# A hybrid attention and linear-attention layer: parts of the columns of w_in kept in DRAM by the first token group

## The chip, the cores and the metric

One Trainium2 chip, one of its cores. The metric is the device time of one execution in microseconds (us), median over runs; the profile is of one further execution.

## What is computed

One layer of a decoder trunk, for 1024 prompt tokens with 16 meta tokens in front of them and for 64 sample tokens (8 sequences of 8). All data are float32. Cut to what matters here:

```python
h = rms_norm(x, norm1)
z = einsum('btd,de->bte', h, w_in)      # w_in: 1024 x 2320
# columns of z: q 512, k 128, v 128, gq 256, gk 256, gv 512, g_low 16, og 512
a = window_attention(rms_norm(q), rms_norm(k), v)   # softmax over 128 keys, 8 heads
o, s = gla_chunked(gq, gk, gv, log_decay(g_low))    # gated linear attention, 4 heads
x = x + concat(a, rms_norm(o) * silu(og)) @ w_o
x = x + swiglu(rms_norm(x), w_gate, w_up, w_down)
```

## The kernel before, in words

**Parts.** TensorE multiplies float32 operands in one pass after each was split in two parts: `hi`, the value rounded to the format fp32r, and `lo`, the rest (`raw - hi`). A product is three matmuls (`mm3`, L102 to L107: hi by hi, hi by lo, lo by hi). Every weight chunk is therefore loaded as `raw`, rounded on ScalarE (`nc.scalar.copy`, L99) and subtracted on VectorE (L100). That is `load_split` (L92 to L101). A chunk of 128 x 1024 has 512 KB, and so has each of its two parts. The tiles `raw` have 3 buffers; `hi` and `lo` have 4 each (`rawpool`, `wpool`) in the stage of this change; a buffer of `hi` and `lo` is free again when the last matmul that reads it is done.

**Token groups.** The tokens are worked on in three groups of 3 tiles (`NG`, `tiles`): group 0 is the sample tokens with the meta tokens and two tiles of the prompt, groups 1 and 2 are three tiles of 128 tokens each. For each group `in_proj(g)` (L348 to L594) runs the input projection in column blocks: kv with g_low (272 columns), gq, gk (256 each), q, gv, og (512 each). q, gv and og are taken in 4 chunks of 256 rows by 512 columns (`token_major`, L366 to L386), gq and gk in 2 chunks of 512 rows by 256 columns each (L490 to L500). So each group loads and splits the same columns of w_in again: 16 chunks without kv. `PAIRS` (L30) takes two chunks at a time, and in turn: (chunk 0, tile 0), (1, 0), (0, 1), (1, 1), (0, 2), (1, 2), and then chunks 2 and 3. The two chunks of a pair thus come free almost together, at the pair's end.

**What sets the order.** `merge` (L978 to L1004) is a planner that runs while the program is built: it interleaves the steps of the input projection, of the output projection, of the attention (`attention_prompt`, L605, and `attention_sample`, L810) and of the linear attention (`gla_prompt`, L705, with `level_factors` at L678, and `gla_sample`, L869), from costs and waits that each step states. TensorE's order is the one that `merge` writes. On the other engines and on the DMA queues the scheduler of the kernel language sets the order when the program is built; each then runs its instructions in that fixed order, and an instruction that waits holds all behind it.

**Queues.** Loads of weights and inputs are issued on SP (`nc.sync.dma_start`, L83 for `raw`, L217 to L220 for the sample tokens' caches and states, L229 for x). GpSimd (POOL) issues a few stores (L442 to L446, L959, L1009 to L1012, L1086), makes the masks of `constants2` (L256) and computes the inverse roots of the norms (`rstd`, L162 to L166). A DRAM pool named `dram` is there already: `kvd` (L234) and `x1d` (L1015) are written and read back.

Of the kernel before, what the change touches and what calls it, by code (L numbers as in the profile page):

```python
# [8 lines left out]
F32 = mybir.dt.float32  # L9
# [8 lines left out]
P = 128  # L18
# [12 lines left out]
LAT = (1.34, 1.18, 1.23, 1.23, 1.2)  # L31
SPARSE, SHARE = 2.0, 1.0
POOL_HALVES = ((0, 1), (1,), (1,))
C_Q, C_K, C_V, C_GQ, C_GK, C_GV, C_GL, C_OG = 0, 512, 640, 768, 1024, 1280, 1792, 1808


@with_exitstack
def hymba_step(ctx: ExitStack, tc: tile.TileContext, x_prompt, x_sample, cache_k, cache_v, state_gla, meta,
               norm1, w_in, q_norm, k_norm, sinks, w_g2, b_g, gla_norm, w_o, norm2, w_gate, w_up, w_down,
               y_prompt, y_sample, nck_p, ncv_p, nst_p, nck_s, ncv_s, nst_s):  # L40
    nc = tc.nc
# [15 lines left out]
    dram = ctx.enter_context(tc.tile_pool(name="dram", bufs=1, space=bass.MemoryType.DRAM))  # L57

    def big(name):
        return psb.tile([P, 512], F32, tag="big", name=name)  # L60
# [4 lines left out]
    w_in_v = w_in.rearrange("(k p) e -> p k e", p=P)  # L65
# [10 lines left out]
    def load_raw(srcs, nk, n, name):  # L76

        raw = (rawpool[-1] if nraw[0] % 4 == 3 else rawpool[0]).tile([P, 1024], F32, tag="raw", name=f"raw_{name}")
        nraw[0] += len(rawpool) > 1
        c = 0  # L80
        for s in srcs:
            w = s.shape[-1]
            nc.sync.dma_start(raw[:, 0:nk * n].rearrange("p (k e) -> p k e", k=nk)[:, :, c:c + w], s)  # L83
            c += w
        return raw

    def parts(name):
        pool = wpool[nsplit[0] % 10 >= 4] if len(wpool) > 1 else wpool[0]
        nsplit[0] += len(wpool) > 1
        return (pool.tile([P, 1024], F32R, tag="hi", name=f"hi_{name}"),  # L90
                pool.tile([P, 1024], F32R, tag="lo", name=f"lo_{name}"))

    def load_split(srcs, nk, n, name, raw=None):

        if raw is None:
            raw = load_raw(srcs, nk, n, name)
        hi, lo = parts(name)
        raw_, hi_, lo_ = (a[:, 0:nk * n].rearrange("p (k e) -> p k e", k=nk) for a in (raw, hi, lo))
        nc.scalar.copy(hi_, raw_)  # L99
        last_lo[0] = nc.vector.tensor_tensor(lo_, raw_, hi_.bitcast(F32), op=ALU.subtract)  # L100
        return hi_, lo_  # L101

    def mm3(ps, lhs, rhs, first, last):
        (lh, ll), (rh, rl) = lhs, rhs
        nc.tensor.matmul(ps, lh, rh, start=first, stop=False)  # L105
        nc.tensor.matmul(ps, lh, rl, start=False, stop=False)  # L106
        nc.tensor.matmul(ps, ll, rh, start=False, stop=last)  # L107

    def mm2(ps, lhs, rhs, first, last):

        nc.tensor.matmul(ps, lhs, rhs[0], start=first, stop=False)
        nc.tensor.matmul(ps, lhs, rhs[1], start=False, stop=last)
# [38 lines left out]
    def tiles(g):  # L151
        return [3 * g - 1 + i for i in range(3)]
# [195 lines left out]
    def in_proj(g):  # L348

        hi8, hi, lo = hT[0][:, :, 0:P], hT[0][:, :, 64:], hT[1]  # L350
# [15 lines left out]
        def token_major(pieces, n, name, ps, order, after=None, sample_only=False):  # L366

            ps.extend(big(f"{name}{i}")[:, 0:n] for i in range(3))
            w = {}
            for step, (b, i) in enumerate(order):  # L370
                if b not in w:
                    w[b] = kv_w.pop(0) if kv_w else load_split([s[:, 2 * b:2 * b + 2, :] for s in pieces], 2, n, name)
                wh, wl = w[b]
                sl = slice(i * P, i * P + P)
                for k in range(2):
                    kk = 2 * b + k
                    rhs, ends = (wh[:, k, :], wl[:, k, :]), (kk == 0, kk == KC - 1)
                    if sample_only and g == 0 and i == 0:
                        mm2(ps[i], hi8[:, kk, :], rhs, *ends)
                    else:  # L380
                        mm3(ps[i], (hi[:, kk, sl], lo[:, kk, sl]), rhs, *ends)
                yield 6 * n / 2400.0
                if step % 3 == 2 and pend:
                    yield from pend.pop(0)
                if after:
                    yield from after(b, i)  # L386

        def into_hT(x, i, pool=()):
            sl = slice(i * P, i * P + P)
            for hf in range(2):  # L390
                transposed(x[i], P, n1T, hi[:, :, sl], lo[:, :, sl], (hf,), pool)
                if g == 0 and x is xt and i == 0:
                    ks = slice(hf * 4, hf * 4 + 4)
                    nc.gpsimd.tensor_copy(hi8[:, ks, 0:64], lo[:, ks, 0:64])
                yield 0.45

        kv_w = []
        if g == 0:
            for i, t in enumerate(tiles(g)):
                normed(xt[i], xt[i], P, f"1_{t}")  # L400
                if i == 0:
                    next(cols1)
                yield from into_hT(xt, i, POOL_HALVES[i])
                if i < 2:
                    kv_w.append(load_split(None, 2, 272, "kv", kv_raw[i]))
# [5 lines left out]

        ps = []
        yield from token_major(kv_src, 272, "kv", ps, PAIRS)
        GR[g]["lokv"] = last_lo[0]
        kns, gls, rks = [], [], []
# [74 lines left out]
        for nm, c0 in (("gq", C_GQ), ("gk", C_GK)):  # L490
            ps = [big(f"{nm}{pr}")[:, 0:384] for pr in range(2)]
            for k0 in range(0, KC, 4):
                wh, wl = load_split([w_in_v[:, k0:k0 + 4, c0:c0 + 256]], 4, 256, nm)
                for pr in range(2):
                    bs = slice(pr * P, pr * P + P)
                    for k in range(4):
                        mm3(ps[pr], (wh[:, k, bs], wl[:, k, bs]), (hi[:, k0 + k, :], lo[:, k0 + k, :]),
                            k0 + k == 0, k0 + k == KC - 1)
                    yield 12 * 0.163
                if pend:  # L500
                    yield from pend.pop(0)
            for i, t in enumerate(tiles(g)):
                yield need(lambda: done["G"] >= t + 2 - 4)
                a = R[t][nm] = work.tile([P, 2, P], F32, tag=nm, bufs=4, name=nm)
                for pr in range(2):
                    p1 = ps[pr][:, i * P:(i + 1) * P]
                    if nm == "gq":
                        nc.scalar.activation(a[:, pr, :], p1, AF.Copy, scale=0.125)
                    else:
                        nc.scalar.copy(a[:, pr, :], p1)  # L510
# [4 lines left out]

        ps = []
        yield from token_major([w_in_v[:, :, C_Q:C_Q + 512]], 512, "q", ps, PAIRS, sample_only=True)
        qns, rqs = [], []
        rows = [slice(0, 64 if t < 0 else P) for t in tiles(g)]
# [37 lines left out]

        ps = []
        yield from token_major([w_in_v[:, :, C_GV:C_GV + 512]], 512, "gv", ps, PAIRS)
        for i, t in enumerate(tiles(g)):  # L560
            yield need(lambda: done["G"] >= t + 2 - 3)
            gv = R[t]["gv"] = work.tile([P, 512], F32, tag="gv", bufs=3, name="gv")
# [8 lines left out]
        def after(b, i):  # L571
            if b == 3 and g < NG - 1:
                yield from into_hT(GR[g]["xnext"], i)
# [9 lines left out]
        for i, t in enumerate(tiles(g)):  # L583
            x, s = ps[i], sg[rows[i], i, :]
# [505 lines left out]
    def projections():  # L1090
        for g in range(NG):
            yield from in_proj(g)
            done["P"] += 3
# [430 lines left out]
    for c, pairs in enumerate(CHUNKS):  # L1524
        first, last = c == 0, c == len(CHUNKS) - 1
        W = W + blocks_W((1,)) if first else blocks_W(pairs)
        for tp in range(4):
# [6 lines left out]
            for j, m in enumerate(DOWN):  # L1534
# [6 lines left out]
                a = Y[tp][m]  # L1541
# [57 lines left out]
```

## Time and profile before

| | |
|---|---|
| median of 3 runs | 1252.57 us (1247.94 to 1252.75) |
| the profiled execution's own time | 1251.81 us |
| its span, first to last instruction | 1250.0 us |
| mean granted clock of TensorE | 0.985 of full |
| instructions | 23188 |
| DMA over the span | 183.17 MB |

The page gives for each engine its busy time and share of the span. Matmuls are pipelined: a matmul counts as busy from its start to its modelled end, so that several overlap, and an idle time of TensorE in the trace is a real stop. The three input projections stand at about 17 to 118 us (group 0), 124 to 251 us (group 1) and 254 to 373 us (group 2); attention and linear attention run in between.

### The profile page before, as it was taken

The numbers are of one execution on the slowest core, as the hardware profiler recorded it, in microseconds if no ns is written. First come the engines' busy times: TensorE is split into PE (matmuls) and PEld (weight loads), VectorE is DVE, ScalarE is ACT, GpSimd is POOL, SyncE is SP. The second block draws the span as 40 slices with busy tenths as digits, with TensorE's granted clock in tenths as the row PEclk, the third lists the DMA queues.
The fourth block names the chain that finished last, engine by engine and source line by source line (L and its number), as shares of the span: only waits on it lengthen the run. The fifth ranks groups of instructions, "written<-read, shape, count | busy, mean of one in ns | idle before, by whom it ended". The sixth has DMA issues, their size and how long they took to land.

```text
span 1250.0 us, 23188 instructions
## 1 busy us (share of the span) xinstructions
PE 1202.7 (96%) x9190; PEld 1066.3 (85%) x9190; DVE 873.2 (70%) x1742; ACT 514.7 (41%) x933; POOL 415.7 (33%) x360
## 2 busy tenths in 40 slices
PE   6999899999999999899999999999999979999997
PEld 6877788778777778789999999999999958888886
DVE  6746987698679876756667656666666666667786
ACT  5634665566566454433234323333332344112200
POOL 6212202131211101215434443544354433334653
PEclk9998999999999999989999999999999999999999
DMA  6723423242323544314435434442544486576545
GB/s 186 237 79 92 121 69 94 54 123 86 101 69 100 165 170 154 116 51 137 128 113 170 154 97 143 154 146 85 180 137 127 147 311 260 211 268 253 213 182 177
DMA packets 145178, 183.17 MB, mean 147 GB/s; under 512 B 15675, under 2 KB 113374, under 8 KB 145054
## 3 DMA queue, kind: packets, MB, share of 16 engines
q1 hardware_dynamic: 95438, 130.83, 32.0%
q10 hardware_dynamic: 47792, 43.98, 10.9%
q0 software_dynamic: 1840, 6.88, 1.6%
q8 instruction: 72, 1.18, 0.4%
q14 instruction: 36, 0.29, 0.1%
HBM read 131.86 MB, written 50.86 MB: 146 GB/s over the span
## 4 chain that ended last, share of the span: by engine, by line
PE 52%; issue 20%; POOL 13%; DVE 8%; ACT 4%; DMA 2%; SPq 0%; POOLq 0%; ACTq 0%; DVEq 0%
PE pd L106 6%; PE pd L107 5%; PE pd L105 5%; PE pw L105 2%; PE pw L106 2%; PE pw L107 2%; POOL raw_wu L1267 2%; PE pf L107 2%; PE pf L105 1%; PE pf L106 1%; POOL raw_wg L1265 1%; ACT hi_wg L1246 1%; PE gv L105 1%; DVE uo L1247 1%; POOL raw_wg L1264 1%
## 5 line engine op out<-in xcount | busy, mean ns | idle before, releaser
L105 PE MATMUL pd<-hi_wd,u 128*128 128x512 f32 x312 | 122.7, 393 | 5.0 <-ACT hi_wd L1246 5.0
L106 PE MATMUL pd<-lo_wd,u 128*128 128x512 f32 x312 | 123.4, 396 | 1.5 <-DVE lo_wd L1247 1.5
L107 PE MATMUL pd<-hi_wd,u 128*128 128x512 f32 x312 | 122.5, 393 | 0.0
L1246 ACT CAST hi_wg<-raw_wg 128x1024 fp32r<-128x1024 f32 (+1 forms) x44 | 41.4, 942 | 139.5 <-PE pf L106 65.9
L1247 DVE TENSOR_TENSOR uo<-u,uo 128x512 fp32r<-128x512 f32 x74 | 77.7, 1056 | 25.4 <-ACT uo L1246 24.0
L1543 DVE TENSOR_TENSOR y<-y,pd 128x512 f32<-128x512 f32 x112 | 73.5, 682 | 27.1 <-PE pd L107 27.1
L1247 DVE TENSOR_TENSOR lo_wu<-raw_wu,hi_wu 128x1024 fp32r<-128x1024 f32 (+1 forms) x44 | 49.2, 1119 | 55.8 <-ACT hi_wu L1246 55.8
L1246 ACT CAST hi_wd<-raw_wd 128x1024 fp32r<-128x1024 f32 x42 | 43.0, 1051 | 97.6 <-PE pd L107 38.4
L1246 ACT CAST uo<-u 128x512 fp32r<-128x512 f32 x74 | 44.7, 620 | 80.1 <-POOL u L1371 39.4
L105 PEld LDWEIGHTS pd<-hi_wd,u 128*128 128x128 f32 x312 | 58.9, 189 | 19.2 <-ACT hi_wd L1246 5.9
L106 PEld LDWEIGHTS pd<-lo_wd,u 128*128 128x128 f32 x312 | 59.0, 189 | 15.3 <-DVE lo_wd L1247 2.8
L1264 POOL TENSOR_TENSOR raw_wg<-raw_wg 128x512 f32<-128x512 f32 x11 | 18.4, 1669 | 160.6 <-DVE lo_wg L1247 135.4
L107 PEld LDWEIGHTS pd<-hi_wd,u 128*128 128x128 f32 x312 | 59.0, 189 | 12.6
L1247 DVE TENSOR_TENSOR lo_wg<-raw_wg,hi_wg 128x1024 fp32r<-128x1024 f32 (+1 forms) x44 | 48.9, 1112 | 27.8 <-ACT hi_wg L1246 27.8
L1247 DVE TENSOR_TENSOR lo_wd<-raw_wd,hi_wd 128x1024 fp32r<-128x1024 f32 x42 | 61.1, 1466 | 7.8 <-ACT hi_wd L1246 7.7
L1246 ACT CAST hi_wu<-raw_wu 128x1024 fp32r<-128x1024 f32 (+1 forms) x44 | 41.3, 938 | 52.9 <-POOL raw_wu L1265 28.4
L590 POOL TENSOR_SCALAR sg<-sg 128x512 f32<-128x512 f32 (+1 forms) x9 | 14.1, 1564 | 133.9 <-ACT sg L589 133.9
L106 PE MATMUL pw<-lo_wo,hThi 128*128 128x512 f32 x128 | 51.2, 400 | 2.7 <-DVE lo_wo L100 2.7
L105 PE MATMUL pw<-hi_wo,hThi 128*128 128x512 f32 x128 | 52.2, 408 | 0.0
L107 PE MATMUL pw<-hi_wo,hTlo 128*128 128x512 f32 x128 | 50.9, 398 | 0.0
L1264 POOL TENSOR_TENSOR raw_wu<-raw_wu 128x512 f32<-128x512 f32 x11 | 14.2, 1291 | 91.6 <-DVE lo_wu L1247 91.6
L1410 ACT ACTIVATE g<-g 128x544 f32<-128x544 f32 x44 | 28.9, 657 | 22.8 <-DVE g L1300 18.9
(714 smaller groups left out, 4248.4 us busy)
## 6 DMA issues: line engine op xcount, KB each, us to landing
ud<-uo ACTq DMA_DIRECT2D x74, 512.0 KB, 4.4
u<-ud SPq DMA_DIRECT2D x40, 896.0 KB, 6.2
raw_wo<-in_w_o_dram SPq DMA_DIRECT2D x24, 512.0 KB, 3.8
raw_wu<-in_w_up_dram SPq DMA_DIRECT2D x22, 512.0 KB, 3.8
raw_wg<-in_w_gate_dram SPq DMA_DIRECT2D x22, 512.0 KB, 4.5
raw_wd<-in_w_down_dram SPq DMA_DIRECT2D x22, 512.0 KB, 4.1
raw_q<-in_w_in_dram SPq DMA_DIRECT2D x12, 512.0 KB, 5.0
raw_gv<-in_w_in_dram SPq DMA_DIRECT2D x12, 512.0 KB, 3.6
```

The source lines that it names most:

```text
L105: nc.tensor.matmul(ps, lh, rh, start=first, stop=False)
L106: nc.tensor.matmul(ps, lh, rl, start=False, stop=False)
L107: nc.tensor.matmul(ps, ll, rh, start=False, stop=last)
L590: nc.gpsimd.tensor_scalar(s, s, 2.0 ** 60, None, op0=ALU.min)
L1246: nc.scalar.copy(hi, src)
L1247: nc.vector.tensor_tensor(lo, src, hi.bitcast(F32), op=ALU.subtract)
L1264: nc.gpsimd.tensor_tensor(a22, a21, a22, op=ALU.add)
L1265: nc.gpsimd.tensor_tensor(a21, a11, a21, op=ALU.subtract)
L1267: nc.gpsimd.tensor_tensor(a12, a12, a11, op=ALU.subtract)
L1410: nc.scalar.activation(a, a, AF.Silu)
L1543: tt(a, a, ps, op=ALU.add)
```

## The change

Group 0 loads and splits its chunks as before, and then also stores both parts of 16 of them (q, gv, og: 4 chunks each; gq, gk: 2 each) to tiles in DRAM, with DMAs that GpSimd issues. Groups 1 and 2 don't load `raw` for these chunks and don't split: they load the two parts straight into buffers of `hi` and `lo`, with DMAs on SP. The chunks of kv are treated as before, and so is w_o. The diff, whole:

```diff
+KEPT = ("q", "gv", "og")
...
-    def load_split(srcs, nk, n, name, raw=None):
-
+    kept = {}
+
+    def load_split(srcs, nk, n, name, raw=None, key=None):
+
+        if key in kept:
+            hl = parts(name)
+            for a, d in zip(hl, kept[key]):
+                nc.sync.dma_start(a[:, 0:nk * n].bitcast(F32), d)
+            return tuple(a[:, 0:nk * n].rearrange("p (k e) -> p k e", k=nk) for a in hl)
         if raw is None:
             raw = load_raw(srcs, nk, n, name)
         hi, lo = parts(name)
         raw_, hi_, lo_ = (a[:, 0:nk * n].rearrange("p (k e) -> p k e", k=nk) for a in (raw, hi, lo))
         nc.scalar.copy(hi_, raw_)
         last_lo[0] = nc.vector.tensor_tensor(lo_, raw_, hi_.bitcast(F32), op=ALU.subtract)
+        if key:
+            kept[key] = [dram.tile([P, nk * n], F32, name=f"{key}{i}") for i in range(2)]
+            for a, d in zip((hi, lo), kept[key]):
+                nc.gpsimd.dma_start(d, a[:, 0:nk * n].bitcast(F32))
         return hi_, lo_
...
-                    w[b] = kv_w.pop(0) if kv_w else load_split([s[:, 2 * b:2 * b + 2, :] for s in pieces], 2, n, name)
+                    w[b] = kv_w.pop(0) if kv_w else load_split([s[:, 2 * b:2 * b + 2, :] for s in pieces], 2, n, name,
+                                                                            key=f"{name}{b}" if name in KEPT else None)
...
-                wh, wl = load_split([w_in_v[:, k0:k0 + 4, c0:c0 + 256]], 4, 256, nm)
+                wh, wl = load_split([w_in_v[:, k0:k0 + 4, c0:c0 + 256]], 4, 256, nm, key=f"{nm}{k0}")
```

## Rows read from the trace of the kernel before

**Rows 1.** The page, section 1: TensorE's busy time, share of the span, instructions.
```profile
PE 1202.7 (96%) x9190; PEld 1066.3 (85%) x9190; DVE 873.2 (70%) x1742; ACT 514.7 (41%) x933; POOL 415.7 (33%) x360
```

**Rows 2.** Busy time by stretch: length; PE, PEld, DVE, ACT, POOL; PEclk; DMA share; GB/s.
```profile
20.00:50.00 30.00, 29.66 (x176) 27.36 (x176) 22.83 (x79) 21.33 (x49) 9.55 (x16) 1.00 0.97 299
50.00:85.00 35.00, 35.00 (x203) 28.26 (x202) 19.86 (x40) 17.28 (x29) 8.99 (x9) 1.00 0.37 105
85.00:112.00 27.00, 27.00 (x221) 21.33 (x219) 13.71 (x40) 6.93 (x17) 2.02 (x1) 0.81 0.23 60
112.00:160.00 48.00, 43.11 (x527) 36.39 (x527) 42.14 (x145) 31.58 (x79) 14.67 (x18) 0.96 0.39 115
160.00:240.00 80.00, 80.00 (x799) 63.76 (x801) 58.00 (x194) 44.04 (x100) 9.63 (x12) 1.00 0.26 75
240.00:290.00 50.00, 46.92 (x564) 39.30 (x553) 45.70 (x163) 37.78 (x100) 16.17 (x17) 1.00 0.34 102
290.00:375.00 85.00, 85.00 (x859) 68.07 (x858) 62.52 (x206) 47.97 (x105) 10.82 (x12) 1.00 0.29 88
```

**Rows 3.** Waits of TensorE, 112 to 380 us: us in total, times, longest.
```profile
PE pa L741 <- DVE Dt L692: 1.4, 1, 1.4
...
PE pk L458 <- DVE AD L702: 0.6, 1, 0.6
PE pst L770 <- DVE mx L623: 0.5, 1, 0.5
PE pk L458 <- ACT glT L455: 0.4, 1, 0.4
...
PE pgl L454 <- DVE mx L623: 0.4, 1, 0.4
PE pb L759 <- DVE Dt L692: 0.4, 1, 0.4
```

**Rows 4.** VectorE in order of time, 138 to 153 us: start, us, instruction.
```profile
138.22 1.21 DVE L100 TENSOR_TENSOR lo_gq<-raw_gq,hi_gq 128x1024 fp32r<-128x1024 f32 x1
139.35 0.27 DVE L690 TENSOR_TENSOR qd<-Dt,gq 128x128 f32<-128x128 f32 x1
...
146.91 1.22 DVE L100 TENSOR_TENSOR lo_gk<-raw_gk,hi_gk 128x1024 fp32r<-128x1024 f32 x1
...
151.28 1.22 DVE L100 TENSOR_TENSOR lo_gk<-raw_gk,hi_gk 128x1024 fp32r<-128x1024 f32 x1
```

**Rows 5.** Busy time by stretch, one stretch of group 1 (columns as in Rows 2).
```profile
154.00:157.40 3.40, 3.40 (x13) 2.96 (x13) 3.34 (x14) 0.67 (x3) 0.00 (x0) 0.50 0.42 137
```

**Rows 6.** ScalarE's instructions of line 99 from 112 to 375 us: min, median, max ns.
```profile
L99 ACT CAST hi_q<-raw_q x8: 1044/1046/1058, 148.2 to 302.6; 128x1024 fp32r<-128x1024 f32 x8
```

**Rows 7.** The tile hi_q of group 0: ns min, median, max; first and last start.
```profile
L111 PE MATMUL q<-hi_q,hThi x8: 389/389/397, 47.8 to 56.4; 128*128 128x512 f32 x8
...
L100 DVE TENSOR_TENSOR lo_q<-raw_q,hi_q x4: 1219/1225/1226, 40.4 to 49.9; 128x1024 fp32r<-128x1024 f32 x4
```

**Rows 8.** ScalarE in order of time, at 138 us.
```profile
137.94 0.84 ACT L687 ACTIVATE Dt<-Dt 128x768 f32<-128x768 f32 x1 [0.26 <-DVE Dt L686]
```

**Rows 9.** The page, section 3, GpSimd's DMA queue: packets, MB, share of 16 engines.
```profile
q0 software_dynamic: 1840, 6.88, 1.6%
```

**Rows 10.** The tile x1d: issues on GpSimd of 512 KB stores, ns min, median, max.
```profile
L1086 POOL DMA_DIRECT2D x1d<-xr x8: 531/608/640, 424.8 to 512.8; - x8
```

**Rows 11.** SP in order of time, one load of a raw chunk.
```profile
22.77 0.37 SPq L83 DMA_DIRECT2D raw_gq<-in_w_in_dram  x1
```

**Rows 12.** DMA issues from 0 to 400 us: count, KB each, median us to landing.
```profile
raw_q<-in_w_in_dram SPq DMA_DIRECT2D x12, 512.0 KB, 5.0
raw_gv<-in_w_in_dram SPq DMA_DIRECT2D x12, 512.0 KB, 3.6
```

**Rows 13.** The tile hi_gv of group 2: its last matmuls' row (columns as in Rows 7).
```profile
L107 PE MATMUL gv<-hi_gv,hTlo x24: 387/390/398, 323.6 to 343.7; 128*128 128x512 f32 x24
```

**Rows 14.** GpSimd in order of time, 59 to 62 us.
```profile
59.84 0.20 POOL L164 TENSOR_SCALAR rq<-msq 128x8 f32<-128x8 f32 x1 [7.03 <-DVE msq L533]
...
61.86 1.83 POOL L164 TENSOR_SCALAR rq<-msq 128x8 f32<-128x8 f32 x1
```

## The prediction

> **What bounds the kernel now.** I began with the page: TensorE is busy 96% of the span, every other engine 70% or less [rows 1]. So a change that only unloads VectorE and ScalarE can pay no more than the stops of TensorE that they cause, in the stretches where their work goes. Second, I read busy time by stretch [rows 2]. From 50 to 112 us (most of group 0), from 160 to 240 and from 290 to 375 us TensorE never stops, whatever VectorE does. It stops in two stretches, the starts of groups 1 and 2: 48.00 - 43.11 = 4.9 us from 112 to 160, and 50.00 - 46.92 = 3.1 us from 240 to 290. There VectorE is nearly full (42.14 of 48 and 45.70 of 50). These 8.0 us, with the clock that they may cost, are the most that the change can win where it removes work. Third, the waits of TensorE from 112 us on [rows 3] say which chains end last: the level factors of the linear attention, the score maxima, the copies in front of the transposes. Fourth, VectorE's order of time shows what of the removed work stands in front of them [rows 4]. Last, the DMA share by stretch: in group 0 the engines are 97% busy from 20 to 50 us, then 37% and 23% [rows 2]. That is where the added stores must go.
>
> A measurement of this kernel can tell about 0.5%, 6.3 us, from no change.
>
> **What the change removes.** Groups 1 and 2 drop 16 chunks each: 32 casts of 1.05 us [rows 6], 33.5 us of ScalarE, and 32 subtractions of 1.22 us [rows 7], 39 us of VectorE. Most of that lies in stretches where TensorE doesn't stop and is worth nothing: matmuls cover it already.
>
> In the start of group 1 it counts. At 138.22 a subtraction of gq takes 1.21 us just before the level factors for which TensorE then stops 1.4 us [rows 3, 4]. ScalarE had finished their exponential at 137.94 + 0.84 = 138.8 [rows 8], VectorE went on at 139.35 [rows 4], so only 0.6 us of the 1.4 comes back; the rest is the chain itself. Next, two subtractions of gk, at 146.91 and 151.28, stand in front of maxima, copies and predicated copies [rows 4] behind which TensorE stops for 0.4 (pb), 0.5 (pst), 0.4 (pgl), 0.4 (pk after glT) and 0.6 us (pk after AD): 2.3 us [rows 3]. As 2.4 us of work goes from in front of them, I count all 2.3. The sum is 2.9 us. The bounds are 0 (POOL's roots or ScalarE turn out later) and all 8.0.
>
> **The clock.** Right behind these stops, from 154.0 to 157.4 us, the granted clock is 0.5, which is 1.2 GHz of 2.4 [rows 5]. 3.4 us at half speed cost 1.7 us. Without most of the stops I count these as won: 1.7, with bounds 0 and 1.7. The stop of 3.1 us at the start of group 2 has no removed work that I can place in front of it, and I count nothing there.
>
> **What it adds in group 0.** 32 stores of 512 KB. The nearest price is GpSimd's own queue: 6.88 MB took 1.6% of 1250 us, 20 us, so 512 KB take 1.52 us of all 16 engines [rows 9], and 32 take 49 us. From 50 to 112 us there are 0.63 x 35 + 0.77 x 27 = 43 us free [rows 2], enough for the 24 parts of q, gv and og (36.5 us). The eight parts of gq and gk (12.2 us) are made before those of q, whose first subtraction is at 40.4 us [rows 7]; from 20 to 50 us only 0.03 x 30 = 0.9 us is free [rows 2]. Loads of q that stand in the same stretch come later, by at most 12.2 - 0.9 = 11.3 us. The cover is the lead of the split: lo_q is done at 40.4 + 1.2 = 41.6 us, and TensorE first uses q at 47.8 [rows 7], 6.2 us later. So the end of the path moves by between 0 and 5.1 us. The 97% speaks for the upper end. For the lower end speaks that the last four of these parts are only made when the loads of q are on their way, so that part of the stores falls behind them. I take the middle, 2.5 us, and keep both ends.
>
> The Trainium skill, page "DMA: Bandwidth & Descriptors", section "Issuing engines are not separate DMA queues", says that DMAs issued by different engines run on the same 16 DMA engines and interleave, so that another issuer buys no bandwidth. By that rule alone the term is its upper end, 5.1 us, and the sum comes out at 1253.1; were the stores on engines of their own it would be 0 and 1248.0. No row of the kernel before has a large store of GpSimd beside a full load queue.
>
> **Buffers and queues.** A buffer of hi and lo is now also held until its store has landed. The casts of q reuse the buffers of gq and gk. A cast that waits for a store holds all behind it on ScalarE (exponentials, evacuations), and VectorE's subtraction and then TensorE wait for it; the same 6.2 us cover it, and it is in the term above. GpSimd issues a 512 KB store in 0.61 us [rows 10]: 19.5 us for 32, beside 9.55 + 8.99 + 2.02 = 20.6 us of work in 92 us [rows 2]. Behind a store that waits for VectorE stand only the roots of the norms; TensorE, which does not stop from 50 to 112 us, covers some of that delay. I count 0; the bounds are 0 and 0.6 us, one issue. SP issues 64 loads of parts for 32 raw loads, 0.37 us each [rows 11]: 12 us more over 250 us of an engine that only issues, 0.
>
> **Loads of parts.** They may start only when TensorE has freed a buffer; before, a raw chunk could be loaded ahead of that. In the densest block, gv of group 2, the 4 chunks last from 323.6 to 343.7 us [rows 13], 10 us a pair. The next pair but one is four loads: 3.6 us for the first to land [rows 12] and 3 x 1.52, 8.2 us. It fits, with 1.9 us to spare: 0, with the bound below as a rival. A load that waits on SP holds the raw loads of kv and w_o behind it; these are wanted a block later.
>
> **The sum.** -2.9 - 1.7 + 2.5 = -2.1 us on the profiled execution: 1251.8 - 2.1 = 1249.7. Its span is 1250.0, with 1.8 us around it, and its time lies 0.8 below the median of the runs, 1252.6. Against that median: **1250.5 us**.
>
> **Rivals.** *1. More comes back.* VectorE and ScalarE being lighter throughout, both stops vanish (8.0) with the half-clock stretch (1.7), and the stores hide: 1252.6 - 9.7 = 1242.9. For it: VectorE is 88% and 91% busy in just these stretches. Against: stops before 138 us and at the start of group 2 come with chains that no removed subtraction precedes. Chance 0.28.
>
> *2. Slower: the stores hold the buffers.* The place is group 0. The first q is 5.1 us late, and from 50 to 85 us the demand is 0.37 x 35 = 13 us of loads, 16 stores of 1.52 = 24.3 and 5.1 carried over: 42.4 in 35, another 7.4. Then 1252.6 - 4.6 + 12.5 = 1260.5. It decides when the stores are served ahead of loads rather than in their gaps; against it speaks that the stops would move TensorE's need later too. Chance 0.16.
>
> *3. Slower: parts come late in groups 1 and 2.* If the first load lands in 5.0 us, as those of q do [rows 12], and the other three share with the 29% that others use [rows 2], a pair takes 5.0 + 3 x 1.52 / 0.71 = 11.4 us for 10: 1.4 late, at some 8 changes of pair in gv and og: 11 us, 1261.5. It decides above 10 us a pair. Chance 0.09.
>
> *4. GpSimd's issues stretch beside VectorE.* A small operation of GpSimd took 0.20 us at 59.84 and 1.83 us at 61.86, the same form [rows 14]. Were each store 1.6 us later in that way, the two parts of a chunk would free its buffer 3.3 us later: 1250.5 + 3.3 = 1253.8. Chance 0.05. The Trainium skill, page "SBUF — State Buffer", section "Who interferes with whom", has such a lock: GpSimd writes the descriptors of its DMAs through ports that VectorE can hold for a whole instruction. The pair of rows agrees with a delay of some kind, but shows no DMA.
>
> **How the numbers follow.** The forecast has 0.42. Faster than 1246.3: most of rival 1 and a little of the forecast's lower side, 0.29. Slower than 1258.9: most of rivals 2 and 3, 0.21. In between 0.50. The range goes from just under rival 1's time to just above rivals 2 and 3, 1242 to 1263; the forecast's own range is 1246 (no cost of stores, and 2 us more won than counted) to 1258 (5.1 paid, nothing won).
>
> **What would show it.** Right: no hi and lo work of q, gq, gk, gv, og after 120 us on ScalarE and VectorE; TensorE's idle time from 112 to 160 us near 2 us; DMA full from 20 to about 60 us; first q near 50 us instead of 47.8; no waits for DMA in groups 1 and 2. Wrong: waits of ScalarE's casts or TensorE for GpSimd's stores over 6 us in total, or TensorE waiting for loaded parts; or, on the other side, a first q still at 47.8 and both starts free of stops.

## The result, and the profile after

| | before | after |
|---|---|---|
| median | 1252.57 us (1247.66 to 1257.31, 5 runs beside it) | **1262.65 us** (1261.25 to 1264.94, 5 runs) |
| the profiled execution | 1251.81 us, span 1250.0 | 1262.65 us, span 1260.9 |
| mean granted clock | 0.985 | 0.984 |

The ratio after to before is **1.0089** [1.0071, 1.0108]: about 10 us slower. The forecast was 1250.5; the time lies near the upper end of the range.

The page first: sections 1 and 3, which answer to [rows 1] and [rows 9].

```profile
PE 1204.8 (96%) x9190; PEld 1066.1 (85%) x9190; DVE 838.2 (66%) x1710; ACT 483.6 (38%) x901; POOL 423.7 (34%) x392
...
q0 software_dynamic: 6448, 23.66, 4.9%
```

The change does what it says. VectorE and ScalarE have 32 instructions less each (1742 to 1710, 933 to 901) and 35 and 31 us less work; GpSimd has 32 issues more. GpSimd's queue moved 23.66 MB instead of 6.88: 16.78 more, the 32 stores of 512 KB. TensorE does the same work, so its 10 us are stops or clock. Busy time by stretch says where (columns as in [rows 2]):

```profile
20.00:50.00 30.00, 27.47 (x155) 25.15 (x155) 14.19 (x57) 12.71 (x32) 11.69 (x20) 0.94 1.01 354
50.00:85.00 35.00, 27.40 (x112) 20.06 (x110) 21.04 (x43) 17.33 (x31) 19.06 (x29) 0.97 0.94 342
85.00:112.00 27.00, 25.80 (x228) 20.31 (x228) 13.20 (x42) 10.10 (x23) 4.83 (x10) 0.92 0.77 266
112.00:160.00 48.00, 44.34 (x427) 37.45 (x426) 34.98 (x107) 26.68 (x73) 13.52 (x19) 0.91 0.50 165
160.00:240.00 80.00, 79.77 (x758) 65.04 (x757) 45.86 (x188) 33.26 (x91) 8.40 (x12) 0.99 0.45 158
240.00:290.00 50.00, 47.60 (x705) 38.61 (x704) 41.40 (x160) 29.09 (x79) 9.86 (x14) 1.00 0.40 132
```

Read it beside [rows 2]. From 50 to 85 us TensorE was busy 35.00 of 35 us and is now busy 27.40: a stage that never stopped loses 7.6 us. The DMA share there was 0.37 and is now 0.94; from 85 to 112 us it was 0.23 and is 0.77. The loss lies in group 0 and goes with full DMA engines. The next view counts what these moved from 20 to 85 us (packets, MB, rate; then by queue: packets, MB, share of 16 engines). Before:

```profile
DMA packets 10784, 12.67 MB, mean 195 GB/s; under 512 B 756, under 2 KB 7274, under 8 KB 10778
...
q1 hardware_dynamic: 10650, 12.46, 63.9%
```

After:

```profile
DMA packets 12558, 22.59 MB, mean 348 GB/s; under 512 B 764, under 2 KB 6720, under 8 KB 12553
...
q1 hardware_dynamic: 9261, 10.87, 51.4%
q0 software_dynamic: 3292, 11.67, 45.8%
```

The engines moved 1.8 times as much and were full, and yet the loads (q1) got 1.6 MB less than before: stores and loads shared, and the loads fell behind. Single transfers show the same. These are DMA issues of the kernel after, 17 to 112 us (count, KB each, median us from issue to landing, where the view pairs them):

```profile
raw_q<-in_w_in_dram SPq DMA_DIRECT2D x4, 512.0 KB, 12.5
q<-hi_q POOLq DMA_DIRECT2D x4, 512.0 KB, 8.2
...
raw_gv<-in_w_in_dram SPq DMA_DIRECT2D x4, 512.0 KB, 9.6
```

In the same stretch of the kernel before, raw_q took 6.8 us and raw_gv 3.6. Who waits for these loads is seen on ScalarE, 58 to 70 us of the kernel after (start, us, instruction, and in brackets the idle time before it and what ended it):

```profile
58.65 1.05 ACT L107 CAST hi_q<-raw_q 128x1024 fp32r<-128x1024 f32 x1 [1.92 <-DMA raw_q<-in_w_in_dram]
...
64.78 1.06 ACT L187 ACTIVATE junk<-x 128x1024 bf16<-128x1024 f32 x1 [4.35 <-DMA x<-in_x_prompt_dram]
...
66.56 1.03 ACT L107 CAST hi_gv<-raw_gv 128x1024 fp32r<-128x1024 f32 x1
68.41 1.04 ACT L107 CAST hi_gv<-raw_gv 128x1024 fp32r<-128x1024 f32 x1 [0.82 <-DMA raw_gv<-in_w_in_dram]
69.36 0.57 ACT L535 COPY q<-q 64x512 f32<-64x512 f32 x1
```

A cast of q, the Square of the next group's x and a cast of gv wait for DMAs in turn, and the evacuation of q stands behind them. TensorE's waits, 20 to 140 us (us in total, times, longest), name what came late:

```profile
PE tq L563 <- DVE qn L552: 2.5, 1, 2.5
PE gv L117 <- DVE qn L552: 2.3, 1, 2.3
PE pk L471 <- DVE vcol L149: 1.9, 1, 1.9
PE gv L118 <- DVE lo_gv L108: 1.6, 1, 1.6
PE pss L841 <- DVE mT L833: 1.2, 1, 1.2
```

None names a DMA: TensorE waits for VectorE, VectorE for ScalarE or GpSimd's roots, those for ScalarE, ScalarE for a load. Followed matmul by matmul (TensorE's order is the same in both kernels), the kernel after is 2.7 us late at the first q (50.48 instead of 47.76), 5.3 at the first gv, 15.4 at 85 us and 16.0 at 140. After that it gains: 13.9 at 157 us, 11 to 12.6 at 381, and 10.9 at the end of the span. So **some 16 us were lost in group 0, and some 5 won behind it**.

### The profile page after: what moved, and what is told of

The parts are those of the page before. It is cut to its first block, busy times and chain, and to the rows that moved or that the text cites. A ratio compares the mean times of both kernels' runs of the same rounds, so it can differ in the third digit from the quotient of the medians.

```text
span 1260.9 us, 23202 instructions
## 1 busy us (share of the span) xinstructions
PE 1204.8 (96%) x9190; PEld 1066.1 (85%) x9190; DVE 838.2 (66%) x1710; ACT 483.6 (38%) x901; POOL 423.7 (34%) x392
## 3 DMA queue, kind: packets, MB, share of 16 engines
q0 software_dynamic: 6448, 23.66, 4.9%
## 4 chain that ended last, share of the span: by engine, by line
PE 48%; issue 21%; POOL 14%; DVE 8%; ACT 4%; DMA 3%; SPq 0%; POOLq 0%; ACTq 0%; DVEq 0%
PE pd L118 5%; PE pd L119 5%; PE pd L117 5%; PE pw L117 2%; PE pw L118 2%; PE pw L119 2%; POOL raw_wu L1280 2%; ACT hi_wg L1259 2%; POOL raw_wg L1278 1%; PE pf L119 1%; PE pf L117 1%; PE pf L118 1%; POOL raw_wg L1277 1%; DVE uo L1260 1%; POOL u L1389 1%
## 5 line engine op out<-in xcount | busy, mean ns | idle before, releaser
L1259 ACT CAST uo<-u 128x512 fp32r<-128x512 f32 x74 | 44.7, 619 | 79.0 <-POOL u L1384 39.3
```

The source lines that it names most:

```text
L1259: nc.scalar.copy(hi, src)
```

## The experiments

Each line: the kernel (diffs are against the kernel after, unless said), median, and ratio to runs of the kernel before on the same chip.

| | parts stored | us | ratio |
|---|---|---|---|
| stores only | group 0, not used | 1268.47 | 1.0131 [1.0112, 1.0149] |
| small stores | group 0, 1/16, not used | 1252.5 | 0.9995 [0.9981, 1.0008] |
| half bytes | group 0, 1/2, not used | 1257.49 | 1.0039 [1.0014, 1.0064] |
| bytes without hold | as stores only, other source | 1268.32 | 1.0145 [1.0119, 1.0172] |
| loads of parts only | 2 of 32 | 1249.14 | 0.9974 [0.9963, 0.9985] |
| gq and gk only | 8 of 32 | 1255.24 | 1.0041 [1.0024, 1.0058] |
| q, gv, og only | 24 of 32 | 1251.98 | 1.0012 [0.9996, 1.0028] |
| stored in group 1 | 32, twice measured | 1248.96, 1249.99 | 0.9973 [0.9964, 0.9981], 0.9994 [0.998, 1.0009] |
| og early | og in group 0, the rest in 1 | 1249.65 | 0.9992 [0.9977, 1.0007] |
| other loads later | 32 | 1258.4 | 1.0066 [1.0041, 1.0091] |
| ScalarE's order | 32 | 1261.34 | 1.0083 [1.007, 1.0095] |

**Stores only.** Group 0 stores; groups 1 and 2 load raw and split as before.

```diff
-        if key in kept:
+        if False:
...
-        if key:
+        if key and key not in kept:
```

> Group 0 stores the parts as in the change, groups 1 and 2 load and split raw chunks as before; the result is the reference's. Both theories of the loss put it into group 0, so both expect the loss without the gain: first gv of group 0 near 67 us, the last og of group 0 near 132 us as in the change (117.8 before), no gain from 150 us on, and a time 1 to 3 us above that of the change: ratio to the kernel before 1.009 to 1.012. If the loss were in the loads of parts of groups 1 and 2, the ratio would be 1.000 to 1.002.

1.0131, a little over its forecast: the stores alone cost 16 us. Against it the whole change stands 1268.47 - 1262.65 = 5.8 us better (5.3 by the ratios), which is what groups 1 and 2 give back.

**Small stores.** As above, with the same 32 issues in the same places and 1/16 of the bytes.

```diff
-                nc.gpsimd.dma_start(d, a[:, 0:nk * n].bitcast(F32))
+                nc.gpsimd.dma_start(d[:, 0:64], a[:, 0:64].bitcast(F32))
```

> As the run with stores only, but each of the 32 stores moves 1/16 of its bytes: the same issues and waits in GpSimd's queue, 1 MB instead of 16.8. Theory 'bytes' (the stores fill the DMA engines, so that loads of q, gv and x land late and ScalarE's casts wait for them): the loss is gone, last og of group 0 at 118 to 120 us, ratio 0.999 to 1.002. Theory 'queue' (the roots of the q norms stand behind stores in GpSimd's queue, and TensorE waits for the normed q): some 7 of the 15 us stay, last og of group 0 near 125 us, ratio 1.004 to 1.007.

0.9995: no loss. The issues on GpSimd, and the waits of the roots behind them, cost nothing that can be measured; the bytes do. The loads land as before (DMA issues, 17 to 112 us, of the small stores):

```profile
raw_q<-in_w_in_dram SPq DMA_DIRECT2D x4, 512.0 KB, 7.0
raw_gv<-in_w_in_dram SPq DMA_DIRECT2D x4, 512.0 KB, 3.6
```

**Half bytes.** The same with half of each part.

```diff
-                nc.gpsimd.dma_start(d, a[:, 0:nk * n].bitcast(F32))
+                nc.gpsimd.dma_start(d[:, 0:512], a[:, 0:512].bitcast(F32))
```

> As the run with the stores alone (1.0131, some 16 us over before), but each store takes the first 512 of its 1024 columns, half the bytes; the 32 issues on GpSimd, their places and the loads are as there. If the loss grows with the bytes in proportion, half of it is left: about 8 us, ratio 1.006 to 1.007. If only what exceeds the free share of the DMA engines and the lead of the loads counts, less than half is left: the eight early stores need 6.1 us of all 16 engines instead of 12.2, of which some 4 us seem to be covered (the loss by them was about 8 us), so 2 us and what follows from them, 1 to 4 us, ratio 1.001 to 1.003.

1.0039 lies between the two forecasts, and its interval reaches into both. By the ratios half the bytes cost 30% of the loss by all (0.0039 of 0.0131), which leans to a cost that starts above a free share; it doesn't show it.

**Bytes without the hold.** As stores only, but a part's store takes 64 columns of it, and the other 15/16 of the bytes come from a tile that nothing waits for (`mflat[0]`, cleared at the start and otherwise unused then).

```diff
-                nc.gpsimd.dma_start(d, a[:, 0:nk * n].bitcast(F32))
+                small = nc.gpsimd.dma_start(d[:, 0:64], a[:, 0:64].bitcast(F32))
+                with tc.issue_after(small.ins):
+                    nc.gpsimd.dma_start(d[:, 64:], mflat[0][:, 1600:2560])
...
+    nc.vector.memset(mflat[0][:, 1536:2560], 0.0)
```

> Stores only, as in the run with the ratio 1.0131, but 15/16 of each store's bytes come from a part of the tile mT0 that is not in use, and only 1/16 from the part's own buffer: as many bytes in the DMA engines, the buffers of hi and lo free early. What is stored is not the parts; nobody reads it, and the outputs are the reference's. Theory 'late loads': no better, ratio 1.011 to 1.014. Theory 'held buffers': the loss goes, ratio 1.000 to 1.004.

1.0145, no better than 1.0131. But the run tests the hold only weakly. The small stores stand in GpSimd's queue among the large ones and still took 3.9 to 6.5 us to land (medians by tile), where whole parts took 5.0 to 8.5 in stores only. DMA issues, 17 to 112 us:

```profile
q<-lo_q POOLq DMA_DIRECT2D x4, 32.0 KB, 6.5
```

Its trace also has a loss that stores only lacks: at 30 us, with the first store just issued (28.3 us), TensorE is already 4.9 us behind the kernel before, as its wait for a normed x grew from 1.9 to 4.3 us. From 30 to 140 us it falls behind by another 13.3 us; stores only falls behind by 16.6 there. So most of the loss stays when buffers come free earlier; up to some 3 us may belong to the hold.

**Loads of parts only.** Only the two parts of the first chunk of gq are stored; groups 1 and 2 load these for every chunk, so they compute with the wrong columns, at the full cost of the loads.

```diff
-            kept[key] = [dram.tile([P, nk * n], F32, name=f"{key}{i}") for i in range(2)]
-            for a, d in zip((hi, lo), kept[key]):
+            first = next(iter(kept.values()), None)
+            kept[key] = first or [dram.tile([P, nk * n], F32, name=f"{key}{i}") for i in range(2)]
+            for a, d in zip((hi, lo), () if first else kept[key]):
```

> Groups 1 and 2 load two parts per chunk as in the change, but only the first chunk of gq is stored, and all loads read its two parts; so the projections of these groups are of wrong weights, with the same shapes and bytes loaded. My theory: group 0 as before (last og at 117.8 us within 1 us), then a gain of 2 to 4 us at the start of group 1 and about 1 us at that of group 2, and no wait for loaded parts: ratio 0.996 to 0.998. Rival: parts come late in groups 1 and 2 and cost about what the lighter VectorE gains: ratio 0.999 to 1.003.

0.9974: 3.2 us faster. The loads of parts cause no wait, and the unloaded engines pay. Group 0 is not as before, though, as had been expected: its last og is 2.3 us late. So its trace also shows what two stores do in the full stretch. TensorE's waits, 20 to 112 us:

```profile
PE pk L472 <- DVE kn L447: 2.7, 1, 2.7
```

No load of a weight ends this stop. A small store on GpSimd's queue (`kvd<-v`, 32 KB) took 6.1 us to land instead of 3.8; GpSimd waits for it before it issues the next DMA, and the root for the last norm of k stands behind that issue. GpSimd:

```profile
32.91 0.61 POOL L1026 DMA_DIRECT2D out_dram<-kvd  x1 [1.97 <-DMA kvd<-v]
33.60 0.19 POOL L177 TENSOR_SCALAR rk<-msk 128x2 f32<-128x2 f32 x1
```

Matmul by matmul it is 3.4 us behind the kernel before at 140 us, 0.5 ahead at 157 and 1.6 ahead at 282. So the start of group 1 gave 3.9 us and that of group 2 another 1.1. Its granted clock from 112 to 160 us was 1.00, where the kernel before had 0.96 [rows 2]: the stretch at 1.2 GHz of [rows 5] is gone.

**gq and gk only, and q, gv, og only.** In each the other chunks are treated as in the kernel before. The first:

```diff
-KEPT = ("q", "gv", "og")
+KEPT = ()
```

> Only the parts of gq and gk are stored and loaded; q, gv and og are split in every group, as before. If the trouble starts where the DMA engines are already full, these 8 stores carry it: q of group 0 starts 2 to 4 us late (50 to 52 us), and what follows makes up none of it; with the 2 to 3 us that group 1 wins at its start the ratio is 0.999 to 1.002. If instead the 24 later stores carry it, q is at 48 us, last og of group 0 at 118 us, ratio 0.997 to 0.999.

The second:

```diff
-                wh, wl = load_split([w_in_v[:, k0:k0 + 4, c0:c0 + 256]], 4, 256, nm, key=f"{nm}{k0}")
+                wh, wl = load_split([w_in_v[:, k0:k0 + 4, c0:c0 + 256]], 4, 256, nm)
```

> The complement: the parts of q, gv and og are stored and loaded, gq and gk are split in every group. First theory (full engines from 20 to 50 us): without the 8 early stores the 36.5 us of the other 24 find room, last og of group 0 at 118 to 121 us, ratio 0.999 to 1.002. Second theory (the stores of q come while loads of gv and x are still owed): gv of group 0 still late, last og at 126 to 130 us, ratio 1.006 to 1.009.

The eight early parts alone cost 0.41%, though they bring a part of the gain with them: more than was expected. The first q comes 5.3 us late (53.05), but TensorE is as late before it reaches q: it stops for 2.7 us at gk and then runs at half clock (1.2 GHz). The 24 later ones with their gain come out even, as the first theory's ratio had it. They are not free, as the prediction had counted them: in the profiled execution (the longest of its 11 executions) the last og of group 0 is at 122.2 us instead of 117.8. Of the loads of q and gv, those beside the stores land late: raw_q with the early eight, raw_gv with the later ones. DMA issues, 17 to 112 us, first of gq and gk only:

```profile
raw_q<-in_w_in_dram SPq DMA_DIRECT2D x5, 512.0 KB, 11.4
raw_gv<-in_w_in_dram SPq DMA_DIRECT2D x4, 512.0 KB, 3.5
```

Then of q, gv, og only:

```profile
raw_q<-in_w_in_dram SPq DMA_DIRECT2D x4, 512.0 KB, 6.8
raw_gv<-in_w_in_dram SPq DMA_DIRECT2D x4, 512.0 KB, 9.6
```

The two ratios add up to 0.53% over, the whole change has 0.89%. That fits early stores that push the work on into the time that the later ones need; with intervals of 0.16 to 0.19% either way it doesn't show it.

**Stored in group 1.** Group 0 is as before, group 1 stores, only group 2 loads parts.

```diff
-    key=f"{name}{b}" if name in KEPT else None)
+    key=f"{name}{b}" if name in KEPT and g else None)
...
-    key=f"{nm}{k0}")
+    key=f"{nm}{k0}" if g else None)
```

> The stores are moved from group 0 to group 1, where the DMA engines are 26 to 39% busy, and only group 2 loads parts; the result is the reference's. If it is the place of the stores that costs, group 1 takes them without a stop: ratio 0.998 to 1.001, with about 1 us won at the start of group 2. If stores cost by themselves (GpSimd's issue, buffers held until they land), the last og of group 1 comes 3 us or more later than the 251.3 us before, and the ratio is 1.002 to 1.006.

> The version that stores all parts in group 1 and loads them in group 2, once more, beside the one that stores og in group 0: again 0.996 to 0.998 of before. Its trace should show where the gain comes from: if the subtractions that group 2 drops are what counts, TensorE's shift against before falls by 2 to 4 us between 240 and 290 us; if the gain is the clock, half-speed stretches of before between 370 and 400 us are missing.

The loss is gone in both measurements: stores in group 1 cost no more than group 2 gets back. Whether it also beats the kernel before is open: 0.9973 the first time, 0.9994 the second, which missed its forecast. The second trace bears out neither reading in full. TensorE's lead over the kernel before grows by 1.0 us between 240 and 282 us, where 2 to 4 were expected. The half-clock stretch of before near 380 us is missing (granted clock 1.00 instead of 0.94 from 370 to 400 us), but at 420 us nothing won by that is left.

**og early.** og is stored in group 0 (in the trace the issues run from 71 to 88 us, not only after 85), all others in group 1.

```diff
-    key=f"{name}{b}" if name in KEPT else None)
+    key=f"{name}{b}" if name == "og" or name in KEPT and g else None)
...
-    key=f"{nm}{k0}")
+    key=f"{nm}{k0}" if g else None)
```

> Correct version: og's parts are stored in group 0 (8 stores, made after 85 us, where the DMA engines of the kernel before were 23% busy), those of gq, gk, q and gv in group 1; groups 1 and 2 load what is stored by then. If the full stretch from 20 to 50 us is the place that costs, this loses nothing in group 0 and is as fast as the version that stores all in group 1 (0.9973) or up to 0.2% faster. If any store in group 0 costs in proportion to its bytes, 8 of 32 stores cost 4 us: 1.000 to 1.001.

0.9992, beside 0.9994 for the version that stores all in group 1, on the same chip. A quarter of the bytes, in group 0 but behind its full stretch, costs nothing that can be measured. TensorE never stops there (columns as in [rows 2]):

```profile
50.00:85.00 35.00, 35.00 (x205) 28.30 (x204) 19.72 (x41) 17.28 (x29) 12.50 (x16) 1.00 0.57 179
85.00:112.00 27.00, 27.00 (x245) 21.89 (x243) 14.60 (x44) 7.94 (x20) 3.65 (x3) 0.87 0.39 123
```

**Other loads later.** The whole change; the sample tokens' caches and states are issued behind q's last raw load, the next group's x behind the last raw load that the program had written by then.

```diff
-            nc.sync.dma_start(raw[:, 0:nk * n].rearrange("p (k e) -> p k e", k=nk)[:, :, c:c + w], s)
+            last_raw[0] = nc.sync.dma_start(raw[:, 0:nk * n].rearrange("p (k e) -> p k e", k=nk)[:, :, c:c + w], s)
...
-            load_sample()
...
+        if g == 0:
+            with tc.issue_after(last_raw[0].ins):
+                load_sample()
...
-            xnext = GR[g]["xnext"] = [load_x(t) for t in tiles(g + 1)]
+            with tc.issue_after(last_raw[0].ins):
+                xnext = GR[g]["xnext"] = [load_x(t) for t in tiles(g + 1)]
```

> The whole change, and on SP the loads of the sample tokens' caches and states (4, behind the last raw load of q) and of the next group's x (3, behind the raw loads of og that are issued by then) are issued later. They are not needed before about 80 and 110 us. Theory 'late loads': the loads of q and gv no longer stand behind them, last og of group 0 at 120 to 125 us, ratio 1.000 to 1.005. If the stores themselves (buffers, write side) set the pace, the ratio stays at 1.007 to 1.010.

1.0066 [1.0041, 1.0091] lies between the two forecasts, some 3 us less than the whole change by the ratios, and its interval reaches into both. The time doesn't decide. The trace says more. It has a stop that the kernel after lacks, 4.2 us at 29 us, while a subtraction of gk on VectorE waits for its late chunk. From the first q to 85 us TensorE then falls behind by 6.4 us (from 5.4 to 11.8), in the kernel after by 12.7 (from 2.7 to 15.4). In these two profiled executions the loads that were moved thus carried about half of the later loss, and nearly half of what that saved was lost again ahead of q.

**ScalarE's order.** The whole change; on ScalarE the Square of the next x and the casts of gv's chunks 1 to 3 stand behind the squares of q; in the changed kernel they stand ahead of them or between them. In `load_split`, and in the same way at the Square of `normed`:

```diff
-        nc.scalar.copy(hi_, raw_)
+        with tc.issue_after(pin[0]) if pin[0] is not None and name == "gv" and later_gv() else nullcontext():
+            nc.scalar.copy(hi_, raw_)
...
-                nc.scalar.activation(qn[r], ps[i][r], AF.Square)
+                sq = nc.scalar.activation(qn[r], ps[i][r], AF.Square)
+                pin[0] = sq.ins if g == 0 else None
```

> The whole change, with one order on ScalarE altered in group 0: the Square of the next group's x and the casts of gv's chunks 1 to 3 stand behind the evacuation and the squares of q, instead of ahead of them. The stores, the loads and TensorE's order are as in the changed kernel. If the loss comes from ScalarE's fixed order, in which work that has its data waits behind casts and Squares whose loads are late (theory), the roots of q start well ahead of 73 us, TensorE's stops for qn shrink, and 4 to 8 of the 10 us come back: ratio 1.002 to 1.006. If the late data itself is what TensorE ends up waiting for (rival: gv's matmuls need the same late chunks), the stops only move to gv, and the ratio stays at 1.007 to 1.010.

1.0083: the rival's number. The evacuation of q now comes at 64.31 us instead of 69.36, and the stops for qn are gone. In their place TensorE waits for a late chunk of gv. First TensorE's longest wait from 20 to 140 us, then ScalarE:

```profile
PE gv L125 <- DVE lo_gv L115: 5.2, 1, 5.2
```

```profile
64.31 0.57 ACT L543 COPY q<-q 64x512 f32<-64x512 f32 x1
...
69.41 1.04 ACT L114 CAST hi_gv<-raw_gv 128x1024 fp32r<-128x1024 f32 x1 [0.78 <-DMA raw_gv<-in_w_in_dram]
72.86 1.04 ACT L114 CAST hi_gv<-raw_gv 128x1024 fp32r<-128x1024 f32 x1 [2.40 <-DMA raw_gv<-in_w_in_dram]
75.36 1.04 ACT L114 CAST hi_gv<-raw_gv 128x1024 fp32r<-128x1024 f32 x1 [1.46 <-DMA raw_gv<-in_w_in_dram]
```

The order on ScalarE only chose where the delay came out. The data is late.

## Why the prediction was wrong

**What failed** is the step "What it adds in group 0", in the sentence that 43 us are free from 50 to 112 us, "enough for the 24 parts of q, gv and og (36.5 us)". It took a mean over 62 us for a supply at the time of need. The parts of q and gv are made while their neighbours' loads run: by 85 us the trace has 22 stores' worth (11.67 MB at 0.524 each) of the 32. The free share from 50 to 85 us was 0.63 x 35 = 22 us [rows 2], and out of these came also what the eight early stores had pushed on. As an estimate from the trace, a store took 1.34 us of all 16 engines, not 1.52 (45.8% of 65 us for 11.67 MB), so the 22 stores needed 30 us, and [rows 2] leave 0.9 + 22 = 23 free from 20 to 85 us. The engines were to be full to about 60 us; they were 94% busy from 50 to 85 us and 77% from 85 to 112.

The term's first part, the late first q, met its number by luck: 2.7 us measured, 2.5 forecast. The forecast's path was late loads of q. These did land later, but the lead of the split covered it: TensorE was already 2.7 us late at the first matmul of gk (42.0 us instead of 39.3) and no later than that at the first q. The 2.7 us arose at a load that the prediction doesn't name, gk's second chunk. ScalarE's cast waited for it, VectorE's subtraction for the cast, and the last norm of k stands behind that subtraction. TensorE stopped for 1.9 us and then ran 3.4 us at half clock (1.2 GHz). In the kernel after, ScalarE, VectorE, TensorE, and the stretch behind (columns as in [rows 2]):

```profile
31.92 1.04 ACT L107 CAST hi_gk<-raw_gk 128x1024 fp32r<-128x1024 f32 x1 [1.40 <-DMA raw_gk<-in_w_in_dram]
33.00 1.23 DVE L108 TENSOR_TENSOR lo_gk<-raw_gk,hi_gk 128x1024 fp32r<-128x1024 f32 x1 [0.82 <-ACT hi_gk L107]
34.14 0.28 DVE L446 TENSOR_TENSOR kn<-kv,rk 128x128 f32<-128x128 f32 x1
34.57 0.30 PE L471 MATMUL pk<-ident,kn 128*128 128x128 f32 x1 [1.93 <-DVE vcol L149]
...
34.80:38.20 3.40, 3.40 (x13) 3.40 (x12) 1.45 (x8) 0.68 (x3) 0.60 (x2) 0.51 1.05 393
```

The term's second part, what the stores cost behind the first q, was counted as 0 and was 13 us. The measured cost of all stores is 16 us (stores only).

**Rival 2** had the place and the arithmetic: 42.4 us of demand in 35, another 7.4, and 1260.5 as its time. It was to decide if the stores are served ahead of loads rather than in their gaps, and got 0.16. The two queues' bytes show what happens: neither ahead nor in the gaps, but side by side, 51.4% and 45.8% of the engines, and that is enough. Its reason against, that the stops would move TensorE's need later too, did not save it. Its name for the mechanism, held buffers, finds no support: from 12 to 140 us of the kernel after no wait of TensorE, VectorE or ScalarE names the landing of a store, and each DMA that ScalarE waits for is a load. The run that gives the bytes another source agrees, but leaves room for some 3 us.

The Trainium skill, page "DMA: Bandwidth & Descriptors", section "Issuing engines are not separate DMA queues", says that issuers share the engines. The runs agree: 1.0131 with the bytes, 0.9995 with the same issues and 1/16 of the bytes. In the prediction that rule was only tried on the first q, at 5.1 us; the same rule holds for each later load in group 0.

**What was right.** The work removed: 32 casts and 32 subtractions. The size of the gain: 4.6 us were forecast for the start of group 1, stops and clock; loads of parts only shows 3.9 there by the trace, and the whole change is 5.8 better than stores only. In the kernel after, that start itself gave 2.1 us (from 16.0 behind to 13.9); the other 3 came later. The waits for AD, pst, glT, pgl and pb [rows 3] are gone from 112 to 380 us, but that for the level factors, of which 0.6 us were to come back, grew from 1.4 to 2.5 us. Their exponential was done at 153.7 us. In place of the subtraction, norms of k that wait for GpSimd's roots now stand in front of them on VectorE, the case that the prediction had kept for its lower bound:

```profile
155.18 0.29 DVE L446 TENSOR_TENSOR kn<-kv,rk 128x128 f32<-128x128 f32 x1 [0.77 <-POOL rk L177]
155.39 0.28 DVE L703 TENSOR_TENSOR qd<-Dt,gq 128x128 f32<-128x128 f32 x1
```

The half-clock stretch of [rows 5] is gone from its place, but another of about its length stands behind this longer stop:

```profile
157.80:161.00 3.20, 3.20 (x13) 2.06 (x12) 3.15 (x17) 1.22 (x5) 0.00 (x0) 0.50 0.44 156
```

Loads of parts only has the longer stop too, but no such stretch from 112 to 160 us. So the 1.7 us of the clock were not won in the changed kernel. Group 2's start, counted 0, gave about 1 us. With the stores at 16 and the gains at 5 to 6, the sum is +10 to +11 instead of -2.1.

**Rival 1** (1242.9) kept its stops: 48.00 - 44.34 = 3.7 us from 112 to 160 (3.9 from 126 to 174, where the same work runs now) and 2.4 from 240 to 290. **Rival 3** falls: no wait of TensorE in groups 1 and 2 names a loaded part, and loads of parts only is faster than before. **Rival 4** falls for the stores. GpSimd in the kernel after, beside VectorE's work:

```profile
73.05 0.20 POOL L176 TENSOR_SCALAR rq<-msq 128x8 f32<-128x8 f32 x1 [1.98 <-DVE msq L546]
73.32 0.58 POOL L112 DMA_DIRECT2D gv<-lo_gv  x1
...
75.69 1.83 POOL L176 TENSOR_SCALAR rq<-msq 128x8 f32<-128x8 f32 x1
...
80.85 0.53 POOL L112 DMA_DIRECT2D gv<-lo_gv  x1
```

The root's first step shows the pair of 0.20 and 1.83 us again [rows 14], but no issue of a store in this stretch took over 0.66 us. The Trainium skill, page "SBUF — State Buffer", section "Who interferes with whom", has GpSimd blocked while an instruction of VectorE keeps the ports that the two share, which only some of its instructions do; no issue of a store here shows such a wait. Roots do come late (73.05 instead of 59.84), but because their input is.

**What stays open.** How much of the 16 us each late load carries: the half-clock stretches, the order of the loads and the stops overlap, and the two runs that moved loads and casts only moved the stops about or saved a part. The clock is the smaller part: as an estimate from the PEclk column, 20 to 160 us, the kernel after lacks 9.3 us of full clock and the kernel before 7.0 [rows 2]. Open too is a share of GpSimd's issues. Small stores shows that they cost nothing while the loads are on time; in the kernel after one stands between the two steps of a root for which q waits (0.58 us at 73.32), and no run takes that apart.

## What to carry to other kernels

Count added DMA traffic against the free share of the engines in the stretch in which it is issued, with what is pushed on from the stretch before, not against a mean over the stage; and take loads in that stretch as delayed by it, even if nobody waits for the stores themselves. To trade engine work for traffic, put the traffic where the engines are idle: the same 32 stores cost 16 us in group 0, and one group later no more than the loads of parts in group 2 bring. Here a reorder on one engine moved a stop to another place and hardly moved the time, because the data was late. And follow a number that came out right along its path: the first q was as late as forecast, for another reason.

## What the runs showed that was not expected

Two stores of 512 KB in the full stretch (loads of parts only) were enough for a stop of 2.7 us and a lag of 3.4 us that was still there at 140 us: where the DMA engines are 97% busy [rows 2], a transfer of 1.52 us [rows 9] was not hidden, and it came out at a small store on the same queue.

In 7 of the 14 profiled executions TensorE stopped for 2.5 to 5.3 us behind the 113th of the 128 small matmuls of pb in group 1, and waited there for nothing that the profile shows. Two profiles of one kernel, stored in group 1, have the one and the other; TensorE, first measurement (1252.32 us):

```profile
147.43 1.41 PE L772 MATMUL pb<-qd,Dt 64*32 64x16 f32 x113 [0.65 <-DVE Dt L705]
154.10 0.33 PE L772 MATMUL pb<-qd,Dt 64*32 64x16 f32 x15 [5.26 <-issue]
```

and second (1248.10 us):

```profile
147.27 1.47 PE L772 MATMUL pb<-qd,Dt 64*32 64x16 f32 x128 [0.65 <-DVE Dt L705]
```

The two executions differ by 4.2 us, most of it there. Its cause was not looked for. A single profile of this kernel can be off by that much, so small gains should rest on medians. The traces of before, after and loads of parts only, from which gains were read above, do not have this stop.
